# The down projection's Strassen parts in token-major form, with 512-column weight tiles

## The chip, the cores and the metric

The kernel runs on one core of a Trainium2 chip. The time is the device time of one execution in microseconds (us). Each kernel is executed several times, and the median is given. The engines of the core are TensorE (PE in the profile, its weight loads PEld), VectorE (DVE), ScalarE (ACT), GpSimd (POOL) and SyncE (SP), which issues most of the transfers.

## The reference

One decoder layer over 512 tokens of 2048 features in fp32: two token mixers (an MLA branch and a gated delta branch), merged and projected, then a SwiGLU channel mixer with 5632 hidden features, then a last RMS norm. What matters here is the end:

```python
h = _rmsnorm(x, norm_ffn[l]) * (1.0 + sc_f) + sh_f
gate, up = jnp.split(h @ w_gate_up[l], 2, axis=-1)
x = x + gt_f * ((jax.nn.silu(gate) * up) @ w_down[l])
return _rmsnorm(x, final_norm)
```

`gt_f` is one gate value for each of the 2048 output features, the same for all tokens.

## The kernel before, in words

Every fp32 operand is split into a high and a low part of type fp32r (ACT casts the high part, DVE subtracts it from the source for the low part), and a product is three matmuls: high by high, high by low, low by high. All of it accumulates in PSUM banks of 128 x 512 values. PE has a stationary operand of 128 x 128 and a moving one of up to 512 columns.

The channel mixer comes in these stages, in the order of PE. `gu0` and `gu_both` make the first gate and up columns. `big(s)`, s = 1 to 10, makes 512 gate and 512 up columns each, by a seven-product Strassen form in which weights and activations are split in two halves of rows (h) and columns: 16 units, 8 of a first pass with the products m1, m6, m7, m5 (24 matmuls of 128 x 512) and 8 of a second pass with m2, m4, m3 into the same eight PSUM banks (18 matmuls). The stationary operand is a 128 x 128 piece of an activation sum and the moving one a 512-column weight sum, so a result has tokens on its partitions and is called token-major. The second pass needs one weight sum of the first again; it goes through `s_dram`, stored by POOL and loaded by SP. `turned_a` transposes the activated results, between the matmuls of the second pass, to the feature-major form (features on partitions) that the down projection takes.

The down projection has 44 blocks of 128 rows. Blocks 0 to 15 ("ks=0") and 16 to 31 ("ks=1") go by Strassen, blocks 36 to 39 and 40 to 43 by plain feature-major sets (`dn`, called dn36 and dn40 below), blocks 32 to 35 are the last group. The order is dn36, ks=0, dn40, ks=1, last group. `strassen_down(ks, n)`, n = 0 to 3, is feature-major before the change: the stationary operand is a 128 x 128 piece of a weight sum, the moving one 256 columns (tokens) of an activation sum. Each of its 8 units (`strassen`, in `unit(k)`) loads a raw weight tile of 128 x 4 x 256, makes four weight sums on DVE (L1889), splits them and three raw parts (ACT L1897, DVE L1898) and issues 42 matmuls (the seven products, two halves, three each). Each of the two ks takes 32 units or 1344 matmuls. After a set, ACT scales the four results by the gate, with a sign for some (`gt_ffn`, `gt_neg`), and POOL adds them by an accumulating DMA to `x2_dram`, which holds the residual, feature-major.

The activation sums of a ks come from `sums_down(ks)`, a generator in a chain: for each quarter q it loads four tiles from `f_dram`, makes four sums (L1998) and seven high and low splits (L239, L240). `down_ready(ks, q)` draws them before the first matmul of a unit that needs them. The buffers of a quarter come free when the one before of the other ks is gone (`gone`, counted up in the last set of a ks, and `free(q)`).

The order of work is in the class `Driver`. A unit has loads (`start`), a preparation (`split`), matmuls, and work before and after (`pre`, `post`). The driver issues loads and preparations some units ahead. The chains (sums, outputs, activations) are stepped once after each GROUP = 12 matmuls (`pump`), or drawn when needed. PE, SP and POOL issue strictly in the order of the program; DVE and ACT instructions are put in order by the scheduler of the language, by their place and their operands.

The last group: `last_dn` runs the last Strassen set, brings `x2_dram` back into SBUF, and then makes the output in two halves. For tokens 0 to 255 it is feature-major (tiles dnl, 192 matmuls with 256 moving columns): the result is scaled and added (`add_gated`), the squares are summed over partitions by matmuls with a column of ones (hss), the norm's factor is spread by a diagonal matrix (hbc), `finished` writes `out`. For tokens 256 to 511 the residual is transposed (`turned`, tile x2T, 32 transposes), and `token_unit` makes 128 x 512 results (tile dnt, 96 matmuls), multiplies by the gate's row (L2240), adds to the residual (L2241), squares with a sum along the row (ACT L2242), multiplies by the norm's row (L2243); `scaled` applies the factor and writes `out_t`.

## Time and profile before

| | us |
|---|---|
| median of 3 runs | 2760.21 (2759.62 to 2762.45) |
| profiled execution | 2757.97 |
| its span | 2755.9 |
| PE busy | 2726.4 |
| DVE busy | 2017.6 |
| ACT busy | 1168.9 |
| POOL busy | 251.5 |

The span is the time from the first to the last instruction that the profiler recorded; the execution's own time is 2.07 longer. The stages on PE, from the first to the last start of their matmuls: `big` 1484.3 to 2264.0, dn36 2264.2 to 2309.4, ks=0 2309.6 to 2483.4, dn40 2483.5 to 2526.8, ks=1 2527.1 to 2692.5, dnl 2692.6 to 2715.5, the transposes to 2721.2, dnt to 2743.3, and then the end at 2755.9.

How lines of a profile are read here: a group of instructions stands as line, engine, operation, output tile <- input tiles, shapes and count, then the busy time in all and the mean duration of one in ns, then the engine's idle time ahead of them with what ended most of it. A line of the timeline begins with the start and the duration; an idle time just before it and its releaser stand in brackets. Nearly all matmuls are issued from one helper, L155, so they are told apart by their tiles: m is a Strassen product.

### The profile page before, as it was taken

The page shows a single profiled execution, that of the slowest core. Times are in us where ns is not written, and L with a number is a line of the kernel's source. Part 1 is how long each engine was busy: PE and PEld are TensorE (multiplying, and loading weights), DVE is VectorE, ACT ScalarE, POOL GpSimd, SP SyncE. Part 2 cuts the span into 40 slices and gives each one's busy share as a digit, 9 for nine tenths or more (in the row PEclk, how much of TensorE's full clock was granted, in tenths as well). Part 3 has the DMA queues.
Part 4 walks back from the last instruction along what each step waited for, and adds up shares of the span by engine and source line. Part 5 has one row for each costly group of instructions (what it writes and reads, how often), then busy time and mean ns, then how long its engine had stood idle before and what let it go on. Part 6 is the DMA issues. An engine that isn't in the chain of part 4 may idle for free.

```text
span 2755.9 us, 39855 instructions
## 1 busy us (share of the span) xinstructions
PE 2726.4 (99%) x14896; PEld 2348.2 (85%) x14896; DVE 2017.6 (73%) x3193; ACT 1168.9 (42%) x1649; POOL 251.5 (9%) x334
## 2 busy tenths in 40 slices
PE   9999999999999999999999999999999999999998
PEld 7888788888888888888999888888888888998997
DVE  8884657676967547785487877778877867878876
ACT  3443432542344343222373444444444445446545
POOL 0000011102100000001000000000000103113113
PEclk9999999999999999999999999999999999999999
DMA  9996556546754648885464565666565668469565
GB/s 350 313 364 203 152 162 179 190 146 182 211 150 153 203 143 287 306 298 195 158 182 146 189 202 199 207 213 201 200 210 191 213 204 193 115 194 207 123 190 173
DMA packets 308538, 557.93 MB, mean 202 GB/s; under 512 B 39956, under 2 KB 109748, under 8 KB 308216
## 3 DMA queue, kind: packets, MB, share of 16 engines
q1 hardware_dynamic: 259848, 461.09, 51.6%
q0 software_dynamic: 28704, 66.37, 9.3%
q10 hardware_dynamic: 19792, 27.92, 2.9%
q8 instruction: 116, 1.90, 0.3%
q14 instruction: 78, 0.64, 0.1%
HBM read 474.52 MB, written 80.76 MB: 201 GB/s over the span
## 4 chain that ended last, share of the span: by engine, by line
PE 94%; DVE 2%; DMA 2%; issue 1%; ACT 1%; SPq 0%; ACTq 0%; DVEq 0%; POOLq 0%
PE m L155 37%; PE wo L155 6%; PE gb L155 6%; PE v L155 4%; PE gu L155 3%; PE z L155 3%; PE ga L155 3%; PE ya L155 3%; PE k L155 3%; PE dn L155 3%; PE q L155 3%; PE yb L155 3%; PE s L155 3%; PE ckv L155 2%; PE cq L155 2%; PE qk L155 1%
## 5 line engine op out<-in xcount | busy, mean ns | idle before, releaser
L263 ACT CAST hi<-raw 128x1024 fp32r<-128x1024 f32 (+1 forms) x274 | 285.2, 1042 | 666.7 <-DMA raw<-in_w_in_dram 131.2
L264 DVE TENSOR_TENSOR lo<-raw,hi 128x1024 fp32r<-128x1024 f32 (+1 forms) x274 | 337.2, 1232 | 305.4 <-ACT hi L263 291.8
L1722 ACT CAST hi<-raws 128x512 fp32r<-128x512 f32 (+1 forms) x240 | 218.4, 910 | 329.0 <-PE m L155 270.4
L1723 DVE TENSOR_TENSOR lo<-raws,hi 128x512 fp32r<-128x512 f32 (+1 forms) x240 | 247.7, 1044 | 86.5 <-ACT hi L1722 86.3
L155 PE MATMUL m<-xl,hi 128*128 128x256 f32 x896 | 257.1, 287 | 3.8 <-DVE xl L240 3.8
L155 PE MATMUL m<-xh,hi 128*128 128x256 f32 x896 | 256.8, 287 | 3.7 <-ACT xh L239 2.3
L155 PE MATMUL m<-xh,lo 128*128 128x256 f32 x896 | 256.6, 286 | 0.8 <-DVE lo L1898 0.8
L435 DVE CUSTOM_DVE_ANT_0 rawm<-rawm,cbc 128x1024 f32<-128x1024 f32 x192 | 234.1, 1238 | 7.8 <-DMA rawm<-in_w_mod_dram 7.2
L155 PE MATMUL m<-hi,h2h 128*128 128x512 f32 x480 | 190.7, 397 | 0.4 <-DVE euvw L1740 0.3
L155 PE MATMUL m<-hi,h2l 128*128 128x512 f32 x480 | 187.2, 390 | 0.0
L155 PE MATMUL m<-lo,h2h 128*128 128x512 f32 x480 | 186.8, 389 | 0.0
L155 PEld LDWEIGHTS m<-xl,hi 128*128 128x128 f32 x896 | 175.0, 195 | 4.7 <-DVE xl L240 4.7
L155 PEld LDWEIGHTS m<-xh,hi 128*128 128x128 f32 x896 | 175.0, 195 | 4.4 <-ACT xh L239 2.7
L155 PEld LDWEIGHTS m<-xh,lo 128*128 128x128 f32 x896 | 175.2, 196 | 1.0 <-DVE lo L1898 1.0
L1722 ACT CAST hi<-sums 128x1024 fp32r<-128x1024 f32 x80 | 84.2, 1052 | 109.2 <-PE m L155 104.2
L1723 DVE TENSOR_TENSOR lo<-sums,hi 128x1024 fp32r<-128x1024 f32 x80 | 97.8, 1222 | 27.3 <-ACT hi L1722 26.8
L155 PE MATMUL wo<-mh,hi 128*128 128x512 f32 (+1 forms) x320 | 111.2, 347 | 0.0
L155 PE MATMUL wo<-mh,lo 128*128 128x512 f32 (+1 forms) x320 | 110.9, 347 | 0.0
L155 PE MATMUL wo<-ml,hi 128*128 128x512 f32 (+1 forms) x320 | 110.9, 347 | 0.0
L1897 ACT CAST hi<-sums 128x1024 fp32r<-128x1024 f32 x64 | 67.1, 1048 | 99.0 <-PE m L155 76.7
L1898 DVE TENSOR_TENSOR lo<-sums,hi 128x1024 fp32r<-128x1024 f32 x64 | 78.2, 1223 | 39.8 <-ACT hi L1897 39.6
L155 PEld LDWEIGHTS m<-hi,h2l 128*128 128x128 f32 x480 | 90.1, 188 | 19.5
(535 smaller groups left out, 7315.9 us busy)
## 6 DMA issues: line engine op xcount, KB each, us to landing
raws<-in_w_gate_up_dram SPq DMA_DIRECT2D x400, 256.0 KB, 3.5
rawm<-in_w_mod_dram SPq DMA_DIRECT2D x192, 512.0 KB, 5.5
raw<-in_w_in_dram SPq DMA_DIRECT2D x144, 512.0 KB, 4.7
raws<-in_w_down_dram SPq DMA_DIRECT2D x128, 256.0 KB, 4.1
raw<-in_w_o_dram SPq DMA_DIRECT2D x40, 512.0 KB, 4.6
s_dram<-raws POOLq DMA_DIRECT2D x80, 256.0 KB, 2.3
raws<-s_dram SPq DMA_DIRECT2D x80, 256.0 KB, 3.3
rawa<-in_w_in_dram SPq DMA_DIRECT2D x32, 512.0 KB, 4.4
```

The costliest lines, as they stand in the source:

```text
L155: return self.tc.keep_in_program_order(f(*args, **kwargs))
L263: nc.scalar.copy(hi[:], raw[:])
L264: (lo_eng or nc.vector).tensor_tensor(lo[:], raw[:], hi[:].bitcast(F32), ALU.subtract)
L435: r = nc.vector.tensor_tensor_reduce(raw, raw, c, 1.0, 0.0, ALU.mult, ALU.add, parts[:, k, half:half + 1])
L1722: nc.scalar.copy(hi[:], src)
L1723: nc.vector.tensor_tensor(lo[:], src, hi[:].bitcast(F32), ALU.subtract)
L1897: nc.scalar.copy(hi[:], src)
L1898: nc.vector.tensor_tensor(lo[:], src, hi[:].bitcast(F32), ALU.subtract)
```

## The change

`strassen` is now one function for gate/up and down. The down projection's Strassen parts take the form of `big`: activation sums stationary, 512-column weight sums moving, results token-major, two sets (n = 0, 1 of 1024 columns) per ks instead of four, 16 units each. The results are multiplied by the gate's row (`gate_row`, a broadcast load from `g_dram`) on DVE and go to a new array `z_dram` by POOL: plain stores for ks=0, accumulating ones for ks=1. `x2_dram` no longer receives them. In the last set (`last_down`) the residual comes back from `x2_dram`, all of it is transposed between the matmuls of the second pass (`turned_x2`), and the sums in `z_dram` are added by accumulating loads (`z_back`). The last group is token-major for all tokens: two sets of 512 columns for four token tiles each (`tm_set`), then eight `token_unit`s. Its weights have been multiplied by the gate's row beforehand: `gated_weights`, a chain started at `big(1)`, loads the 4 x 4 tiles, multiplies them on DVE, and stores them to `l_dram`. `finished`, the gate's negative and the columns of the last norm are gone, and there is one output array.

Of the diff, shortened:

```diff
-    def big(s):
-        g, u = 512 * s, DFF + 512 * s
+    def strassen(w, g, u, par, operand, ready, second_read, finish, freed, extra=None):
+        wg = w.rearrange("(h k p) n -> k h p n", h=2, p=P)
...
+        FIRST4 = [("m1", 0, 1, "m1"), ("m6", 0, 0, "m6"), ("m7", 1, 0, "m7"), ("m5", 1, 1, "m5")]
+        LAST3 = [("m2", 1, 0, "m1"), ("m4", 0, 0, "m7"), ("m3", 0, 1, "m5")]
...
+    def big(s):
...
+        return strassen(w_gu, 512 * s, DFF + 512 * s, s % 2, operand, ready, second_read, finish, freed,
+                        lambda k: turned_a(k - 1) if 1 <= k <= 4 else [])
+
+    def strassen_down(ks, n, extra=None):
+        tiles, rows = {}, []
+        def ready(q):
+            while made[ks] <= q:
+                drv.step(maker[ks])
+        def second_read(c, t, v, ps):
+            if c == "m2":
+                tiles[0, t] = S("y")
+                nc.vector.tensor_tensor(tiles[0, t][:], ps[:], rows[0][:], ALU.mult)
+            elif c == "m4":
+                tiles[1, t] = S("y")
+                nc.vector.tensor_tensor(tiles[1, t][:], v, ps[:], ALU.add)
+            else:
+                nc.vector.tensor_tensor(v, v, ps[:], ALU.add)
+        def finish(v, up1):
+            accum = dict(accum_op=ALU.add) if ks else {}
+            def out_(h, t, f, y):
+                c0 = 1024 * n + 512 * f
+                nc.gpsimd.dma_start(z_dram[2 * h + t, :, c0:c0 + 512], y, **accum)
+            for t in range(2):
+                out_(0, t, 0, tiles[0, t][:])
+            yield
+            for t in range(2):
+                nc.vector.tensor_tensor(tiles[1, t][:], tiles[1, t][:], rows[0][:], ALU.mult)
+                out_(1, t, 0, tiles[1, t][:])
+            yield
+            for h, x in enumerate((v, up1)):
+                for t in range(2):
+                    nc.vector.scalar_tensor_tensor(x[t], x[t], -1.0, rows[1][:], op0=ALU.mult, op1=ALU.mult)
+                    out_(h, t, 1, x[t])
+                yield
+        def freed(second, q):
+            if n == 1 and second:
+                down[ks][q] = None
+                gone[1 + ks] += 1
...
+        us = strassen(w_dn[2048 * ks:2048 * ks + 2048, :], 1024 * n, 1024 * n + 512, (1 + n) % 2, lambda c, q: down[ks][q][c],
+                      ready, second_read, finish, freed, extra)
+        with_pre([us[10]], lambda: rows.extend(gate_row(2 * n + f) for f in range(2)))
+        return us
+
+    def gate_row(n):
+        row = S("row")
+        side(row[:], g_dram[512 * n:512 * n + 512].partition_broadcast(P))
+        return row
+
+    def gated_weights():
+        for n in range(4):
+            row = gate_row(n)
+            for k in range(4):
+                w = S("wg")
+                side(w[:], w_dn[(LAST + k) * P:(LAST + k + 1) * P, 512 * n:512 * n + 512])
+                yield 4
+                tc.keep_in_program_order(nc.vector.tensor_tensor(w[:], w[:], row[:], ALU.mult))
+                side(l_dram[k, :, 512 * n:512 * n + 512], w[:])
+                w = None
+                yield 4
...
-    def strassen_down(ks, n):
...
-                        nc.scalar.activation(half_of(t, k), half_of(t, k), AF.Copy, scale=(gt_neg if f else gt_ffn)[:, k:k + 1])
-                    nc.gpsimd.dma_start(x2_dram[h, 2 * n + f], t[:], accum_op=ALU.add)
...
-    def strassen(w, c1, c0, products, ready, outputs, freed):
...
+        def x2_back(k):
+            n, h = divmod(k, 2)
+            for q in (2 * n, 2 * n + 1):
+                x2f[h, q] = S("x2")
+                side(x2f[h, q][:], x2_dram[h, q])
+        def turned_x2(k):
+            n, h = divmod(k, 2)
+            box = {}
+            def one(t, j):
+                if j == 0:
+                    box["ps"] = PS("x2T")
+                f = 4 * n + j
+                nc.tensor.transpose(box["ps"][:, tok(j)], half_of(x2f[h, f // 2], f)[:, tok(t)], ident)
+                if j == 3:
+                    x_ = xt[2 * h + t, n] = S("x2t")
+                    nc.scalar.copy(x_[:], box["ps"][:])
+                    if n < 2:
+                        z_back(2 * h + t, n)
...
+        def z_back(t, n):
+            nc.gpsimd.dma_start(xt[t, n][:], z_dram[t, :, 512 * n:512 * n + 512], accum_op=ALU.add)
+        def last_down():
+            weights = [last_weights(n, k0) for n in (2, 3) for k0 in (0, 2)]
+            for i, u in enumerate(strassen_down(1, 1, turned_x2)):
+                if 6 <= i < 14:
+                    with_pre([u], lambda i=i: x2_back(i - 6))
+                if i >= 12:
+                    with_pre([u], lambda i=i: reload_a(LAST + i - 12))
                 yield u
+                if i >= 12:
                     yield weights.pop(0)
...
+            for n in range(2):
+                us = tm_set("dnt", lambda k0, nk, n=n: gated(n, k0), 4, at,
+                            lambda ps, n=n: [summed(t, n, ps[t]) for t in range(NT)], late=True)
+                if n == 0:
+                    with_pre(us, last_rows)
+                yield from us
+            for t in range(NT):
+                for n in (2, 3):
+                    yield token_unit(t, n)
...
+        def summed(t, n, ps):
+            x_, sq = xt[t, n], S("sq")
+            nc.vector.tensor_tensor(x_[:], x_[:], ps[:], ALU.add)
+            nc.scalar.activation(sq[:], x_[:], AF.Square, accum_out=sf[:, t, n:n + 1])
+            (nc.gpsimd if n < 2 else nc.vector).tensor_tensor(x_[:], x_[:], norms[n][:], ALU.mult)
...
+        drv.add(gated_weights())
...
-        for n in range(4):
-            for k, u in enumerate(strassen_down(0, n)):
-                if (n, k) == (3, 2):
+        for n in range(2):
+            for i, u in enumerate(strassen_down(0, n)):
+                if (n, i) == (1, 10):
                     def start():
-                        for i in range(40, 44):
-                            reload_a(i)
+                        for k in range(40, 44):
+                            reload_a(k)
                         maker[1] = drv.add(sums_down(1))
...
-        for n in range(3):
-            yield from strassen_down(1, n)
-        yield from last_dn()
+        yield from strassen_down(1, 0)
+        yield from last_down()
```

More of the change, by code (lines that the diff above doesn't have):

```diff
@@ L349, in post @@
                     drv.hold()
-            return Unit(start, split, mms, pre, post, weight=weight, alone=alone)
+            return Unit(start, split, mms, pre, post, weight=weight, alone=alone, late=late and k0 + nk == kt)
         return [unit(k0) for k0 in range(0, kt, nk)]
@@ L1753, in after, with operand @@
+        return [unit(i) for i in range(16)]
+    def big(s):
+        tiles = {}
+        def operand(c, q):
+            if c in ("m1", "m2"):
+                return h2T[0][q if c == "m1" else 4 + q]
+            return h2T[1][4 + q] if c == "m4" else comb[q][c.replace("m", "x")]
+        def ready(q):
+            while xn[0] <= q:
+                drv.step(xc[0])
+        def second_read(c, t, v, ps):
+            if c == "m2":
                 tiles[0, t] = S("g0")
-                nc.scalar.activation(tiles[0, t][:], ps["m1"][t][:], AF.Silu)
@@ L1811, in block_kernel @@
+    LAST = 32
     turning = []
```

367 lines of the change are left out of this document (97 added, 270 removed).

## The prediction

> **What bounds the kernel now.** I read the page's totals and its chain of waits first, then each engine's busy time by stage, then what TensorE (PE) waits for in the stages that change, and last single instructions for their pitch.
>
> ```profile
> PE 2726.4 (99%) x14896; PEld 2348.2 (85%) x14896; DVE 2017.6 (73%) x3193; ACT 1168.9 (42%) x1649; POOL 251.5 (9%) x334
> PE 94%; DVE 2%; DMA 2%; issue 1%; ACT 1%; SPq 0%; ACTq 0%; DVEq 0%; POOLq 0%
> L155 PE MATMUL m<-xl,hi 128*128 128x256 f32 x896 | 257.1, 287 | 3.8 <-DVE xl L240 3.8
> L155 PE MATMUL m<-hi,h2h 128*128 128x512 f32 x480 | 190.7, 397 | 0.4 <-DVE euvw L1740 0.3
> ```
>
> PE is the bound: 99% busy, 94% of the chain that ends last. So an edit counts by the issue time that it takes from PE, and by the waits that it gives PE. The third and fourth rows show the shapes in question: the down Strassen's matmuls (three groups of 896, 2688 in all) take moving tiles of 256 columns, the gate and up projections' take 512. Their mean durations overlap; what counts is the distance from start to start.
>
> ```profile
> 2400.00 0.28 PE L155 MATMUL m<-xh,hi 128*128 128x256 f32 x1
> 2400.12 0.28 PE L155 MATMUL m<-xl,hi 128*128 128x256 f32 x1
> ```
> ```profile
> 1800.18 0.39 PE L155 MATMUL m<-hi,h2h 128*128 128x512 f32 x1
> 1800.41 0.39 PE L155 MATMUL m<-lo,h2h 128*128 128x512 f32 x1
> 1800.63 0.39 PE L155 MATMUL m<-hi,h2l 128*128 128x512 f32 x1
> ```
>
> A 256-column matmul costs 0.120 us, a 512-column one (1800.63-1800.18)/2, 0.225 to 0.227 with the rounding; the stages of such matmuls keep 0.2267. Two of the narrow ones cost 0.240: 13 ns more for the same columns. Now the stages (span and then busy time of PE, its weight loads, DVE, ACT and POOL, the granted clock, DMA share and GB/s):
>
> ```profile
> 1600.00:1700.00 100.00, 100.00 (x456) 82.83 (x455) 76.45 (x90) 44.71 (x56) 7.58 (x14) 1.00 0.60 199
> 2310.00:2484.00 174.00, 167.93 (x1346) 166.55 (x1345) 139.61 (x207) 84.73 (x116) 19.40 (x25) 0.96 0.61 162
> 2484.00:2527.00 43.00, 43.00 (x191) 35.63 (x190) 32.01 (x47) 27.61 (x45) 17.48 (x16) 1.00 1.05 224
> 2527.00:2692.00 165.00, 162.83 (x1342) 162.37 (x1341) 130.95 (x194) 78.39 (x107) 23.49 (x31) 0.99 0.62 161
> ```
>
> Row 1 is gate/up, the pattern the down projection is to take: PE full, VectorE (DVE) at 76%. Row 2 is the first down Strassen stage (K rows 0 to 2047, "ks=0"): 174.0-1346x0.120 = 12.5 us lost, though PE's idle time is only 6. Row 4 is ks=1: 165.0-1342x0.120 = 4.0 lost. The waits in between:
>
> ```profile
> PE m L155 <- DVE xl L240: 3.8, 4, 1.2
> PE m L155 <- ACT xh L239: 2.3, 2, 1.1
> PE m L155 <- ACT hi L1897: 1.4, 1, 1.4
> ```
> ```profile
> 2331.98 0.39 PE L155 MATMUL m<-xl,hi 128*128 128x256 f32 x1 [1.19 <-DVE xl L240]
> 2335.52 0.58 PE L155 MATMUL m<-xl,hi 128*128 128x256 f32 x1 [0.95 <-DVE xl L240]
> ...
> 2336.33 0.41 PE L155 MATMUL m<-xl,hi 128*128 128x256 f32 x1
> 2336.54 0.41 PE L155 MATMUL m<-xh,lo 128*128 128x256 f32 x1
> ```
>
> The operands xl and xh are the activation sums of the down Strassen, which DVE makes while the first units run. After such stalls matmuls follow at 0.21 instead of 0.120 for 4.9 us (the clock of row 2 is 0.96): a spell loses 4.9x(1-0.120/0.21) = 2.1 us beyond the stall.
>
> **The change part by part.**
>
> *Strassen on PE.* 2688x0.120 = 322.6 us become 1344x0.2267 = 304.7: **-17.9**. The weight load of 0.19 us still fits beside a matmul, as in gate/up. The Trainium skill ("TensorE: Matmul & The Clock Gate", Back-to-back issue gap) has the warm gap as N/2.4 ns plus 2.5 ns, which speaks against this gain: 1344 saved fixed parts of 2.5 ns would be an estimated 3.4 us. The rows above contradict it for this kernel's fp32r stream (13 ns).
>
> *Last group of K rows (4096 up).* Before: 192 narrow matmuls (23.0), the transposes' stage, 96 wide ones:
>
> ```profile
> 2715.50 0.28 PE L155 MATMUL dnl<-ah,wll 128*128 128x256 f32 x1
> 2715.62 1.29 PE L155 MATMUL x2T<-kc,x 128*128 128x128 f32 x10
> ...
> 2719.46 1.94 PE L155 MATMUL x2T<-kc,x 128*128 128x128 f32 x16
> 2721.16 0.48 PE L155 MATMUL dnt<-wlh,ah 128*128 128x512 f32 x1
> ```
> ```profile
> 2743.26 0.39 PE L155 MATMUL dnt<-wlh,al 128*128 128x512 f32 x1
> 2743.69 0.69 DVE L2240 TENSOR_TENSOR dn<-dnt,row 128x512 f32<-128x512 f32 x1 [0.20 <-PE dnt L155]
> 2745.04 0.68 DVE L2241 TENSOR_TENSOR x2t<-x2t,dn 128x512 f32<-128x512 f32 x1
> 2745.81 0.63 ACT L2242 ACTIVATE dn<-x2t 128x512 f32<-128x512 f32 x1
> ```
>
> 23.0+(2721.16-2715.62)+(2743.49-2721.16) = 50.9. After: 192x0.2267 = 43.5 and 64 transposes at (2721.16-2719.46)/16 = 0.106, 6.8: 50.3. **-0.6.** The transposes now stand between the last Strassen set's matmuls; each result needs an ACT copy, and ACT is under half busy there.
>
> *DVE in the two Strassen stages.* DVE works in order, so its spare time per unit says how fast the activation sums come. Pitches by the starts of consecutive instructions:
>
> ```profile
> 2310.81 1.23 DVE L1898 TENSOR_TENSOR lo<-sums,hi 128x1024 fp32r<-128x1024 f32 x1 [2.27 <-ACT hi L1897]
> 2311.96 0.69 DVE L240 TENSOR_TENSOR xl<-a,xh 128x512 fp32r<-128x512 f32 x1
> 2312.56 0.69 DVE L1889 TENSOR_TENSOR sums<-raws 128x512 f32<-128x512 f32 x1
> 2313.16 0.95 DVE L1898 TENSOR_TENSOR lo<-raws,hi 128x768 fp32r<-128x768 f32 x1
> 2314.03 0.42 DVE L1889 TENSOR_TENSOR sums<-sums,raws 128x256 f32<-128x256 f32 x1
> 2314.36 0.68 DVE L240 TENSOR_TENSOR xl<-a,xh 128x512 fp32r<-128x512 f32 x1
> ```
>
> 1.15 us for 1024 columns, 0.60 for 512, 0.87 for 768, 0.33 for 256. Before, a unit is 42 matmuls, 5.04 us, and takes DVE 0.60+2x0.33+0.87+1.15 = 3.28: 1.76 spare. After, a first-pass unit is 24 matmuls, 5.44 us, with three operations of 1024 and one of 512, 4.05: 1.39 spare. A second-pass unit is 18, 4.08 us, with 2.35: 1.73 spare. So the stage as a whole fits, as in row 1, but the spare time is smaller just where the sums are due. One quarter q of a ks's activations is four sums and seven splits: 11x0.60 = 6.6 us, used by first-pass units 2q and 2q+1, so quarter q is due 10.9q us after the stage's start (10.1q before).
>
> *Start of ks=0.* Before lost the 12.5. A walk down the changed program's DVE order with these pitches has q2's second operand ready 29.5 us after the start, due at 25.5: 4.0 late, some 2.2 again for q3, and two half-clock spells of 2.1: 10.4. The count of spare time bears that size out: before, three quarters are 33 operations, 19.9 us, against 6x1.76 = 10.6 spare in the first six units; 9.3 and two spells make 13.5, where 12.5 was lost. Bounds: nothing lost (the sums drawn into spare time), or 16, by that count for the new units: 19.9-6x1.39 = 11.6 and two spells. **-2.1** (-12.5 to +3.5).
>
> *Start of ks=1.* Before, the sums of quarters 0 to 2 came from the long end of ks=0 and the plain stage dn40 (row 3), and PE waited for none. The new order gives less room: the generator of the sums is stepped once every 12 matmuls, so every 2.7 us instead of 1.44, and the buffers of the old quarters come free only in the second pass of the last ks=0 set. By the changed order only q0 is made in dn40; the 19.9 us of q1 to q3 fall into the first six units, with their 8.3 spare. The rest, 11.6, comes late, with one half-clock spell: **+13.7**. Bounds: 9 (units 6 and 7 lend their spare time too, no spell) and 20 (all of it exposed). The skill's page on the clock gate (the same title, Part 1) has half rate only after an idle window of about 3.4 us; with three stalls each under that it would take no spell here, 11.6 instead of 13.7. The stalls above, about 1 us each, did bring one.
>
> *End of ks=1.* Before lost 4.0 there by a late weight DMA (the wait on `hi`). After, the loads of the last set are spread; but x2_dram's return, z_dram's accumulating loads, the reloaded activations and the last weights all come in units 6 to 15: 16.8 MB by the diff in about 50.6 us, 330 GB/s. The crowded 12 us before that late DMA:
>
> ```profile
> DMA packets 1828, 4.33 MB, mean 361 GB/s; under 512 B 257, under 2 KB 777, under 8 KB 1826
> ```
>
> Below that, but near. I take 1.5 lost: **-2.5** (-4 to +8: one late set of loads of two units' length).
>
> *Hidden work.* `gated_weights` is 16 DVE multiplies (9.7 us) over some 350 us of gate/up, where row 1 leaves DVE 23 us of each 100; uncovered it would cost those 9.7. The multiplies by the gate row replace ACT scalings and lie in second passes with 1.73 spare per unit. The sums' 32 transfers into z_dram go from POOL and are read back only in the last set.
>
> *Tail.* The last square starts one DVE multiply and one interleaved operation earlier (L2240 to L2241, 1.35 us): **-1.0** (-1.3 to 0).
>
> Sum: -17.9-0.6-2.1+13.7-2.5-1.0 = **-10.4**. Against the profiled execution (span 2755.9 plus 2.07, 2757.97) 2747.6; the median of the runs lies 2.2 above that execution, so **2750**.
>
> **The rivals.**
> *Smooth* (2728): DVE's sums slip into spare time, both starts lose nearly nothing (2 us in all): -17.9-0.6-12.5+2-2.5-1.0 = -32.5. For it: row 1's full PE at 76% DVE. Against: the 19.9 us of sums against 8.3 spare.
>
> *Slower by the sum's way through DRAM* (2768): the weight sum of a first pass is stored to s_dram by POOL and read back by the second pass, and POOL also carries dn40's accumulating transfers.
>
> ```profile
> x_dram<-y POOLq DMA_DIRECT2D x32, 256.0 KB, 8.0
> s_dram<-raws POOLq DMA_DIRECT2D x80, 256.0 KB, 2.3
> raws<-s_dram SPq DMA_DIRECT2D x80, 256.0 KB, 3.3
> ```
>
> If the store of unit 2 stands behind four such accumulates, it holds its buffer, and the next DVE sum behind it, for up to 8.0+2.3+3.3 = 13.6 us while q1 to q3 also wait in that order: 13.7+13.6+5 for two more half-clock spells = 32.3, against -24.1 for the other terms: +8.2. It decides for slower from a loss of 29.6 at this one place. For it: POOL's queue is in order, and those accumulates are the slowest issues. Against: POOL is 40% busy in row 3.
>
> *Same by crowding in the last set* (2760): loads of the last set come 10 us later in all than forecast. For it 330 against 361 GB/s; against, the window above is a burst of several queues, and the loads are issued units ahead.
>
> *The change doesn't do what it says* (2764): a wide matmul of the down stages costs nearly two narrow ones, 0.2375 instead of 0.2267, and 14.5 of the 17.9 stays away. For it: the overlap that a narrow pair lacks was seen in another stage only. Against: 0.2267 stands in gate/up with the same alternation of operands. (The skill's gap formula above comes to the same saving of 3.4.)
>
> **How the numbers follow.** Forecast 0.45, smooth 0.12, crowding 0.17, slower 0.23, not saved 0.03. 0.2% is 5.5 us, about what a measurement tells from no change: faster below 2754.7, slower above 2765.7. Faster 0.45+0.12, less 0.02 for the forecast's upper edge: 0.55; same 0.17+0.03-0.02: 0.18; slower 0.27 with the upper bounds of the other terms. Range: best bounds -17.9-0.6-12.5+9-4-1.3 = -27.3, 2733; worst -17.9-0.6+3.5+20+8 = +13, 2773: **2732 to 2774**; the forecast's own 2740 to 2756.
>
> **What would show it.** PE's 512-column matmuls in both Strassen stages at 0.2267; losses there of 10 and 14 us (window less count times pitch), waits on `x` sums (L240) in the first six units; the clock under 1 in the first 35 us of each; ks=1's last set without a wait on `hi`; the last group about 50 us; the last square some 1.3 us sooner after the last matmul. Wrong if ks=1's sums are ready before its first unit (then smooth), or if waits on weight sums or z loads lead the list.

## The result, and the profile after

The changed kernel takes 2825.2 us (median of 4 runs, 2820.6 to 2826.5) where the kernel before takes 2759.9 (4 runs): a ratio of 1.0234, 95% interval 1.0216 to 1.0251. The forecast was 2750 within 2732 to 2774, faster; the kernel became 65 us slower. The profiled execution has a span of 2823.0, 67.1 more than before. From the first matmul of each stage to the first of the next, in us:

| stage | before | after | at full pitch, after |
|---|---|---|---|
| up to `big` | 1484.3 | 1488.2 | |
| `big` (gate/up) | 779.9 | 792.1 | |
| dn36, dn40 | 45.4, 43.5 | 45.4, 43.5 | |
| ks=0 | 173.9 | 186.9 | 152.3 |
| ks=1 (after: with 64 transposes) | 165.5 | 210.6 | 159.1 |
| last group | 50.7 | 43.4 | 43.5 |
| from the last matmul's start to the end | 12.7 | 12.9 | |

The differences, +3.9, +12.2, +13.0, +45.0, -7.3 and +0.2, make 67.0. So the loss is in the two Strassen stages and, unexpected, in gate/up. The page's totals and chain, then a list of what PE waited for from gate/up to the end (total, times, longest):

```profile
PE 2727.9 (97%) x13478; PEld 2277.8 (81%) x13478; DVE 2013.9 (71%) x3110; ACT 1144.0 (41%) x1589; POOL 298.4 (11%) x420
PE 74%; DVE 9%; DMA 7%; issue 6%; ACT 1%; POOL 1%; SPq 0%; ACTq 0%; DVEq 0%; POOLq 0%
```
```profile
PE m L155 <- DVE euvw L1733: 19.9, 4, 8.9
PE m L155 <- DVE xl L240: 19.4, 6, 7.7
PE m L155 <- ACT xh L239: 13.7, 6, 3.9
PE x2T L155 <- ACT x2t L2148: 8.9, 2, 8.4
PE m L155 <- DVE lo L1717: 7.0, 5, 2.1
PE m L155 <- DVE sl L2009: 1.2, 1, 1.2
PE m L155 <- ACT sl L2007: 1.1, 1, 1.1
```

PE's share of the chain fell from 94 to 74%, and DMA and DVE came up. Two of the waits hardly stood in the kernel before: `euvw` (DVE's reads of the PSUM banks at the end of a first pass; 0.3 us in all before) and `x2t` (ACT's copy of the transposed residual; none before). The windows of the changed kernel say where (columns as in the prediction):

```profile
2326.00:2364.00 38.00, 26.19 (x102) 20.02 (x100) 27.81 (x33) 16.65 (x23) 7.74 (x9) 0.87 0.72 195
2364.00:2464.00 100.00, 97.09 (x414) 79.46 (x415) 81.12 (x99) 43.27 (x52) 15.55 (x29) 0.96 0.67 209
2464.00:2513.00 49.00, 38.62 (x160) 31.12 (x159) 27.87 (x36) 15.02 (x18) 1.09 (x3) 0.90 0.63 205
2556.00:2617.00 61.00, 42.66 (x161) 32.38 (x160) 46.30 (x59) 25.63 (x36) 8.63 (x12) 0.86 0.66 198
2617.00:2688.00 71.00, 71.00 (x315) 58.76 (x314) 56.45 (x68) 29.04 (x33) 10.98 (x15) 1.00 0.64 181
2688.00:2767.00 79.00, 59.63 (x266) 47.46 (x265) 40.73 (x52) 31.09 (x46) 22.04 (x36) 0.87 0.82 267
```

Row 5, the middle of ks=1, is what the change was to be everywhere: 315 matmuls in 71 us, 0.225 each, PE full. The start of ks=0 (row 1) loses 38-102x0.2267 = 14.9, the rest of its first set and the second's first pass (row 2) 6.1, the pass change of its second set (row 3) 12.7, the start of ks=1 (row 4) 24.5, and the last set (row 6, 202 matmuls and 64 transposes at 0.106) 26.4.

**The starts.** POOL, DVE and PE of the changed kernel at the first stall (start, duration; idle time before, and its releaser, in brackets):

```profile
2328.26 4.96 POOL L155 DMA_DIRECT2D x_dram<-y  x4 [6.17 <-ACT y L2061]
2331.19 2.60 POOL L155 DMA_DIRECT2D s_dram<-raws  x1
```
```profile
2334.30 1.22 DVE L1695 TENSOR_TENSOR sums<-raws,raws 128x1024 f32<-128x1024 f32 x1
2343.26 1.23 DVE L1695 TENSOR_TENSOR sums<-raws,raws 128x1024 f32<-128x1024 f32 x1 [7.75 <-DMA s_dram<-raws]
2344.41 1.28 DVE L1695 TENSOR_TENSOR raws<-sums,raws 128x512 f32<-128x512 f32 x2
2345.61 0.68 DVE L240 TENSOR_TENSOR xl<-a,xh 128x512 fp32r<-128x512 f32 x1
```
```profile
2346.35 0.79 PE L155 MATMUL m<-hi,xl 128*128 128x512 f32 x1 [7.72 <-DVE xl L240]
2346.94 0.63 PE L155 MATMUL m<-hi,xh 128*128 128x512 f32 x1
2347.37 0.63 PE L155 MATMUL m<-lo,xh 128*128 128x512 f32 x1
...
2351.23 0.39 PE L155 MATMUL m<-hi,xl 128*128 128x512 f32 x1
2351.46 0.39 PE L155 MATMUL m<-hi,xh 128*128 128x512 f32 x1
```

The store of a weight sum goes out in POOL's queue behind dn36's four accumulating transfers (`x_dram<-y`; the rows leave the number out of `x2_dram`). It reads one of five raw buffers; DVE's next weight sum wants that buffer and waits 7.75 us; the split xl for PE stands behind it in DVE's order. The list names xl, but what ended last is the store. After the stall the matmuls come at 0.43 for nine of them.

The start of ks=1 repeats it. There the profile names no releaser for DVE's wait ("issue"):

```profile
2571.72 1.22 DVE L1695 TENSOR_TENSOR sums<-raws,raws 128x1024 f32<-128x1024 f32 x1 [9.66 <-issue]
```

By the trace's times of issue and landing it is the store again: it went out at 2558.94 behind dn40's four accumulating transfers and landed at 2571.64. In both cases the four landed one after the other, some 2.7 us apart (2334.32 to 2342.31, 2562.46 to 2570.46), and the store about 1 us behind the last (2343.24, 2571.64).

**The pass change.** DVE and POOL in ks=0's second set:

```profile
2472.76 0.69 DVE L1695 TENSOR_TENSOR raws<-raws,raws 128x512 f32<-128x512 f32 x1 [4.16 <-DMA raws<-in_w_down_dram]
2475.34 0.69 DVE L1695 TENSOR_TENSOR raws<-raws,raws 128x512 f32<-128x512 f32 x1 [1.89 <-DMA raws<-in_w_down_dram]
2475.95 1.22 DVE L1717 TENSOR_TENSOR lo<-raws,hi 128x1024 fp32r<-128x1024 f32 x1
2477.09 1.28 DVE L1739 TENSOR_TENSOR euvw<-euvw,m 128x512 f32<-128x512 f32 x2
2478.28 2.47 DVE L1733 TENSOR_TENSOR euvw<-euvw,m 128x512 f32<-128x512 f32 x4
```
```profile
2455.38 0.54 POOL L155 DMA_DIRECT2D s_dram<-raws  x1 [4.41 <-DVE raws L1695]
2455.91 0.54 POOL L155 DMA_DIRECT2D ah<-a_dram  x1
...
2459.09 0.54 POOL L155 DMA_DIRECT2D ah<-a_dram  x1
```

The first pass's matmuls end at 2469.7. The reads that free their banks (L1739, L1733) need nothing more, but stand behind weight sums of later second-pass units (L1695) that wait for their loads. And the loads are late: POOL has sent the eight reloads of stored activations, which the program has at unit 10, in one go from 2455.9 on, while PE was still in the first pass. PE waited 8.9 us. Gate/up shows the same order, without the reloads, at 1776 us and at 1536 us, where the multiply by the gate's row (`wg`) stands between:

```profile
1536.72 0.69 DVE L1695 TENSOR_TENSOR raws<-raws,raws 128x512 f32<-128x512 f32 x1 [1.81 <-DMA raws<-in_w_gate_up_dram]
1537.33 1.22 DVE L1717 TENSOR_TENSOR lo<-raws,hi 128x1024 fp32r<-128x1024 f32 x1
1538.46 0.68 DVE L1893 TENSOR_TENSOR wg<-wg,row 128x512 f32<-128x512 f32 x1
1539.06 1.27 DVE L1739 TENSOR_TENSOR euvw<-euvw,m 128x512 f32<-128x512 f32 x2
```

**The last set.** The transfers of the changed kernel from 2735 to 2760, and ACT in that stretch:

```profile
DMA packets 3844, 8.84 MB, mean 354 GB/s; under 512 B 463, under 2 KB 463, under 8 KB 3844
```
```profile
2744.14 1.07 ACT L2148 COPY x2t<-x2T 128x512 f32<-128x512 f32 x2
2756.80 1.04 ACT L263 CAST hi<-raw 128x1024 fp32r<-128x1024 f32 x1 [4.05 <-DMA raw<-l_dram]
2757.75 1.07 ACT L2148 COPY x2t<-x2T 128x512 f32<-128x512 f32 x2
```

At 354 GB/s for 25 us the casts of the last weights wait for their loads, the copy of the transposed tiles waits behind a cast, and the next transposes wait 8.4 us for the bank.

### The profile page after: what moved, and what is told of

It is laid out like the page before. It is cut to its first block, busy times and chain, and to the rows that moved or that the text cites. A ratio compares the mean times of both kernels' runs of the same rounds, so it can differ in the third digit from the quotient of the medians.

```text
span 2823.0 us, 37070 instructions
## 1 busy us (share of the span) xinstructions
PE 2727.9 (97%) x13478; PEld 2277.8 (81%) x13478; DVE 2013.9 (71%) x3110; ACT 1144.0 (41%) x1589; POOL 298.4 (11%) x420
## 4 chain that ended last, share of the span: by engine, by line
PE 74%; DVE 9%; DMA 7%; issue 6%; ACT 1%; POOL 1%; SPq 0%; ACTq 0%; DVEq 0%; POOLq 0%
PE m L155 30%; PE wo L155 6%; PE gb L155 6%; PE v L155 4%; PE k L155 3%; PE s L155 3%; PE yb L155 3%; PE q L155 3%; PE z L155 3%; PE gu L155 2%; DMA raws<-in_w_down_dram 2%; PE ya L155 1%; PE qk L155 1%; DMA raw<-in_w_in_dram 1%; DVE lo L1717 1%
## 5 line engine op out<-in xcount | busy, mean ns | idle before, releaser
L1716 ACT CAST hi<-raws 128x1024 fp32r<-128x1024 f32 (+1 forms) x336 | 305.7, 910 | 534.9 <-PE m L155 358.8
L1717 DVE TENSOR_TENSOR lo<-raws,hi 128x1024 fp32r<-128x1024 f32 (+1 forms) x336 | 345.8, 1042 | 118.5 <-ACT hi L1716 117.8
L155 PE MATMUL m<-hi,xh 128*128 128x512 f32 x448 | 182.4, 407 | 27.5 <-DVE euvw L1733 13.8
L155 PE MATMUL m<-hi,xl 128*128 128x512 f32 x448 | 181.4, 405 | 19.4 <-DVE xl L240 19.4
L155 PE MATMUL m<-lo,xh 128*128 128x512 f32 x448 | 180.8, 403 | 7.0 <-DVE lo L1717 7.0
L1695 DVE TENSOR_TENSOR sums<-raws,raws 128x1024 f32<-128x1024 f32 x112 | 136.5, 1219 | 40.7 <-DMA raws<-in_w_down_dram 11.7
L1695 DVE TENSOR_TENSOR raws<-raws,raws 128x512 f32<-128x512 f32 x112 | 76.5, 688 | 89.3 <-DMA raws<-in_w_gate_up_dram 59.3
L155 PEld LDWEIGHTS m<-hi,xh 128*128 128x128 f32 x448 | 88.0, 196 | 49.6 <-ACT xh L239 16.8
L155 PEld LDWEIGHTS m<-hi,xl 128*128 128x128 f32 x448 | 87.6, 196 | 41.6 <-DVE xl L240 23.1
L155 PEld LDWEIGHTS m<-hi,h2h 128*128 128x128 f32 x480 | 90.1, 188 | 25.3 <-DVE euvw L1733 7.8
```

The source lines that it names most:

```text
L155: return self.tc.keep_in_program_order(f(*args, **kwargs))
L1695: add = lambda o, x, y: nc.vector.tensor_tensor(o, x, y, ALU.add)
L1716: nc.scalar.copy(hi[:], src)
L1717: nc.vector.tensor_tensor(lo[:], src, hi[:].bitcast(F32), ALU.subtract)
```

## The experiments

Theories at the start: (1) the store's queue makes the stalls at the starts; (2) DVE's order makes those at the pass changes; (3) POOL's side loads run ahead and make weights late; against these the prediction's own reason, (4) DVE's load of activation sums and their slow generator. First each alone. A time without an interval is of a single execution, and so is every stage's time; these are read to some 4 us, as ten executions of one kernel (e6 below) lie between 2758.3 and 2765.6.

**e1_store_act.** The down stages' stores from ACT's queue:

```diff
-                side(s_dram[par, k], r[:, 0, :])
+                (store or side)(s_dram[par, k], r[:, 0, :])
...
-                      ready, second_read, finish, freed, extra)
+                      ready, second_read, finish, freed, extra, nc.scalar.dma_start)
```

> Only the queue changes that stores the weight sums of the two down Strassen stages to s_dram: ACT's in place of POOL's. Queue theory: in the changed kernel each of the two stages starts with a stall of PE of 7.7 us, because the store of a weight sum stands in POOL's queue behind four accumulating transfers and DVE waits for the buffer that it holds. Without those transfers ahead of it both stalls of 7.7 go, and some of the shorter ones after them: 15 to 30 us less than the changed kernel, 2795 to 2810. Rival, DVE's load of activation sums (the prediction's reason): DVE has too little spare time in the first six units, whatever queue the store takes: both starts still lose 20 us and more, and the time stays within 5 us of 2825.

2809.0, 16.2 less. The stalls of 7.7 became 1.8 and 1.5. ks=0 fell from 186.9 to 176.4, ks=1 only from 210.6 to 206.9: later waits at the start of ks=1 (5.3 us on xh) took part of the place. Told by the first set of a stage (the time from its first to its last matmul's start, less 335x0.2267), the loss fell from 21.4 to 13.9 in ks=0 and from 24.8 to 19.9 in ks=1. Theory 1 holds; it is not the whole of the starts. The Trainium skill ("Trainium Kernel Development and Optimization", Key Constraints) says that transfers from all three queues run on the same 16 DMA engines and that issuing from several engines only saves issue time. The measured 16 us show a second thing that a queue decides: what stands ahead in it.

**e2_pin.** The weight sum of a second-pass unit may not be scheduled ahead of what the program has before it:

```diff
-                add(r[:, 0, :], r[:, 0, :], b[:])
+                tc.keep_in_program_order(add(r[:, 0, :], r[:, 0, :], b[:]))
```

> Only the order on DVE changes: the weight sum of a second-pass unit may not move ahead of what the program has before it, so the reads of the PSUM banks at the end of the first pass come ahead of the sums of the units behind them. Order theory: the PE waits for those reads (4.4 and 1.7 us in gate/up, 8.9 us in ks=0, 4.9 us in ks=1) stand behind sums that wait for weight loads; with the order changed they go and nothing takes their place: 20 to 25 us less, about 2802. Rival, late loads: the loads are late in any case, and PE waits as long for the split weights of the first second-pass unit as it did for the reads: under 8 us less, over 2817.

2788.7, 36.5 less: more than expected. Gate/up is back at 781.0, the waits on euvw are gone, ks=0 is at 173.6, ks=1 at 196.5 (the wait of 8.4 us before the transposes went too, which the theory had not named). DVE at the same pass change:

```profile
2453.33 1.22 DVE L1717 TENSOR_TENSOR lo<-raws,hi 128x1024 fp32r<-128x1024 f32 x1 [2.46 <-ACT hi L1716]
2454.48 1.28 DVE L1739 TENSOR_TENSOR euvw<-euvw,m 128x512 f32<-128x512 f32 x2
2455.67 2.66 DVE L1733 TENSOR_TENSOR euvw<-euvw,m 128x512 f32<-128x512 f32 x4
2458.25 0.69 DVE L1695 TENSOR_TENSOR raws<-raws,raws 128x512 f32<-128x512 f32 x1
```

The reads come ahead of the sum, and nothing waits for a load between.

**e3_sp.** Gate rows, reloads and the residual's return through SP, in the program's place, the reloads one block per unit:

```diff
-                side(x2f[h, q][:], x2_dram[h, q])
+                load(x2f[h, q][:], x2_dram[h, q])
...
-                side(aT[k][i][:].bitcast(F32), a_dram[k - 32, i])
+                load(aT[k][i][:].bitcast(F32), a_dram[k - 32, i])
...
+                if n == 1 and 9 <= i < 13:
+                    with_pre([u], lambda i=i: reload_a(31 + i))
```

> The loads of the gate's rows in the down stages, of the stored activations and of x2_dram go to SP's queue, at the places where the program has them, in place of POOL's; the four reloads for dn40 are spread over four units. Crowding theory: POOL issues these loads long before the units that they belong to, some 2 MB at once, and the weight loads beside them land late: with SP's order the stalls at the pass change of ks=0's second set (1.6 and 9.1 us) and before and at that of ks=1's second set (1.7, 2.2 and 5.3 us) go, 15 to 20 us less, about 2807. Rival, order on DVE: the reads of the banks still stand behind sums of later units, and those loads wait for SP just as long: within 6 us of 2825. A third way: loads in SP's queue hold up the weights behind them, and the time rises.

2798.1, 27 less, more than the 15 to 20 expected: ks=0 at 180.0, ks=1 at 190.3. The pass-change waits shrank (8.9 to 4.9, 4.9 to 1.5) but did not go, and the wait before the transposes fell from 8.4 to 1.3. Theory 3 holds beside theory 2.

**e4_nogate.** The chain `gated_weights` left out:

```diff
-        drv.add(gated_weights())
...
-            return [(lambda r: r[:], l_dram[k0:k0 + 2, :, 512 * n:512 * n + 512].rearrange("k p n -> p k n"))]
+            return plain(w_dn, LAST + k0, 2, 512 * n, 512)
```

> The chain that multiplies the last group's weights by the gate's row is left out, and the last group takes its weights from w_down without the gate: that part of the result lacks the gate. If that chain's loads, stores and multiplies are what costs gate/up its 12 us, the stage goes back to 780 us and the time to some 2813. Rival: the stage's stalls come from the order of DVE at the pass change, which the chain only meets by chance: the stage keeps 5 us or more of the 12.

2811.7, and gate/up at 780.5: all of its 12 us go. With e2_pin the chain stays and 11 of the 12 us go too (PE keeps a wait of 1.2 us on an activation sum of gate/up that e4 does not have). So its 16 multiplies are hidden but for about 1 us; what cost was the order of DVE that the scheduler chose with them in the program, at pass changes that they stand next to. What in the chain led the scheduler to it was not tested.

**e8_pump.** The chains stepped every 6 matmuls from ks=0 on:

```diff
-                if self.count >= GROUP:
-                    self.count -= GROUP
+                if self.count >= self.group:
+                    self.count -= self.group
...
+                        drv.group = GROUP // 2
```

> The changed kernel with the chains stepped every 6 matmuls in place of 12 from ks=0 on and nothing else. By the prediction's reason (the sums of ks=1 are late because their generator is stepped half as often) ks=1's first set loses 8 to 14 us less than the 24 that it loses in the changed kernel, about 2813. By the queue theory the first stall there is the store's and stays, and only the shorter waits shrink: 0 to 6 us less, 2819 to 2825.

2803.3, 21.8 less, more than either expectation: ks=0 at 177.4, ks=1 at 199.6. PE's waits on xl and xh fell from 33.1 to 3.7 us. The prediction's reason is real, at both starts. The first set of ks=1 loses 11.7 us in place of 24.8; these 13 us are within what was expected. That of ks=0 loses 13.1 in place of 21.4, which was not expected. At each start one stall stays, of 4.8 and 7.2 us, on split weights.

**Together.** The three edits (e5), with the faster chains (e6), and with single edits taken back or changed:

> The three edits of the first kernels together: ACT's queue for the stores, the pinned second-pass sums, SP's queue for the side loads. If the three causes are separate, their gains add but for what two of them share (the pass changes in the second sets): the changed kernel less 16, less 36, less some 15 for the loads, about 2757, near the kernel before. If they are one cause seen three times, the time stays near the best of them, 2785 to 2790.

> As the kernel with the three edits, and the chains are stepped every 6 matmuls in place of 12 from ks=0 on, so as often in time as before the change. The prediction's reason for the start of ks=1: stepped twice as often, the sums of more quarters are made before the stage starts, and 8 to 14 us go from that start. Rival: the buffers of a quarter come free too late for that, or a faster chain takes DVE's time at a worse place: within 4 us of the kernel with the three edits.

> As the kernel with the three edits and the faster chains, but the weight sums of the down stages are stored from SP's queue in place of ACT's. If the stores on ACT hold up the casts of the activation sums behind them (PE waits for xh, 2 to 5 us each at both starts with the stores on ACT), those waits go: 5 to 12 us less than the same kernel with the stores on ACT. Rival: the casts wait for sums that DVE makes late, whatever ACT stores: within 3 us. A loss: SP's loads of the next units' weights stand behind a store that waits for DVE.

> As the kernel with three edits and faster chains, less the edit of the stores: they go from POOL again. If the store behind POOL's accumulating transfers costs by itself (some 16 us alone), the two starts show a first wait of 4 to 8 us again and the time is 10 to 18 us above 2760.7. Rival: with the chains faster the sums are ready and the store's lateness is covered: within 5 us.

> As the kernel with three edits and faster chains, less the edit of the side loads: POOL issues them ahead again. If the early loads cost by themselves, the last set shows its waits again (transposes on ACT's copy up to 8 us, split weights 2 us each) and the time is 10 to 16 us above 2760.7. Rival: with the order on DVE pinned they do no harm: within 5 us.

| kernel | us | ks=0 | ks=1 |
|---|---|---|---|
| e5_three | 2772.0 | 167.4 | 184.4 |
| e6_three_pump | 2760.7, ratio to before 1.0001 (0.9991 to 1.0011) | 164.5 | 178.7 |
| e7_spstore (e6, stores on SP) | 2792.9, 1.0118 (1.0101 to 1.0134) | 173.3 | 197.8 |
| e12_pin_sp_pump (e6, stores on POOL) | 2770.8 | 170.2 | 182.5 |
| e13_pin_acts_pump (e6, side loads on POOL) | 2772.6 | 165.6 | 189.3 |

e5 lies 53 below the changed kernel, less than the sum of the three alone (80): the causes overlap. e6 is 11 below e5, 8.6 of it in the two stages (5.7 in ks=1, where 8 to 14 were expected). Taking one edit back costs 10 (stores) and 12 us (side loads), so both still count. Without the stores' edit the first waits at the starts are back (5.7 and 6.5 us), as expected. Without that of the side loads the transposes wait 0.4 us and not the 8 expected; the waits on split weights grew in their place, from 12.5 to 19.9 us. On SP the stores are worse than on POOL: SP's next weight loads stand behind a store that waits for DVE (DVE's wait for weights with its first-pass sums is 37.1 us in all, 19.2 in e6). With all four edits e6 is level with the kernel before.

**What is left.** e6 still loses 12.2 us in ks=0 and 19.6 in ks=1 against full pitch.

*e10_layout* (x2_dram as 16 x 128 x 512, so that accumulating transfers move 2 KB rows):

```diff
-                nc.gpsimd.dma_start(x2_dram[:, k // 2, :, 256 * (k % 2):256 * (k % 2) + 256].rearrange("h p n -> p h n"),
-                                    t[:].rearrange("p (h n) -> p h n", h=2), accum_op=ALU.add)
+                nc.gpsimd.dma_start(x2_dram[k], t[:], accum_op=ALU.add)
```

> As the kernel with three edits and faster chains, but x2_dram is laid out by feature block with all 512 tokens in a row, so that the plain stages' accumulating transfers move 2 KB rows in place of 1 KB rows, and the last set loads 16 tiles of that form. If those transfers crowd the DMA engines at the ends of dn36 and dn40, where DVE waits for the s_dram store's buffer (6.1 us in all) and for weights, each of them lands in some 5 us in place of 7, the starts of both Strassen stages lose 3 to 8 us less, and the time falls to 2753 to 2758, below the kernel before. Rival: what those starts wait for is DVE's own backlog and the size of the pieces does not matter: within 2 us of 2760.7. A loss: the last set's loads come in lumps of four.

2762.1, ratio 1.0008 (0.9998 to 1.0018): no gain; the size of the rows is not it.

*e14_spread* (`yield 8` after each of those transfers in the last sets, `yield 3` after each into z_dram, rows from unit 4):

> As the kernel with three edits and faster chains, and three transfers are moved in time: the accumulating transfers of the last set of dn36 and of dn40 go out one every 8 chain steps, so over the first units of the Strassen stage behind; the down sums go to z_dram one every 3 steps; the gate's rows are loaded from unit 4 on in place of unit 10. If the rest of the loss is weights and s_dram stores that land late among these transfers (PE waits of 2.3 and 1.6 us at the start of ks=1, 4.0 us at that of its second set, 1.9 us in ks=0 behind a gate row that lands late), 8 to 14 us go and the time is 2747 to 2753, below the kernel before. Rival: the DMA engines are full in these stretches whatever the order, and the waits move to the next units: within 3 us of 2760.

2761.8, 1.0009 (1.0000 to 1.0018): the waits moved. The one on the gate's row and that of 4.0 us at the start of ks=1's second set went; one of 2.4 us came at 2366, one of 1.8 before the transposes, and that at the start of ks=1 grew from 1.6 to 3.9.

*e15_no_store* and *e16_no_accum* take a suspect away (shortened):

```diff
-                side(s_dram[par, k], r[:, 0, :])
+                if store is None:
+                    side(s_dram[par, k], r[:, 0, :])
...
-            for dst, src in (((box["r"][:, 0, :], s_dram[par, k]), (box["r"][:, 1, :], wg[k, 1][:, u:u + 512]),
+            for dst, src in (((box["r"][:, 0, :], s_dram[par, k] if store is None else wg[k, 0][:, u:u + 512]), (box["r"][:, 1, :], wg[k, 1][:, u:u + 512]),
```
```diff
-            accum = dict(accum_op=ALU.add) if ks else {}
+            accum = {}
...
-                                    t[:].rearrange("p (h n) -> p h n", h=2), accum_op=ALU.add)
+                                    t[:].rearrange("p (h n) -> p h n", h=2))
```

> As the kernel with three edits and faster chains, but the down stages' weight sums are not stored and reloaded: the second pass loads raw weights of the same size in their place, so that part of the result is wrong, and DVE, PE and the loads do as much as before. If the round trip of the sums is what the two stages still lose (some 30 us over matmuls at full pitch), most of the waits at the starts go and the time falls by 10 to 20 us, to 2741 to 2751. Rival: DVE's own load at the starts, or the loads of weights, hold PE as long: less than 5 us.

> As the kernel with three edits and faster chains, but the plain stages' results and those of ks=1 overwrite x2_dram and z_dram in place of being added by the transfer: the same bytes go out, and the residual and ks=0's sums are missing from the result. If accumulating transfers crowd the DMA engines at the starts and at ks=1's second set, those waits shrink and the time falls by 6 to 15 us. Rival: the size of the traffic, not its kind, or DVE's load: less than 4 us.

2743.1 (ks=0 159.7, ks=1 164.9) and 2747.5 (159.7, 171.4): 17.6 and 13.2 less. Both count, and overlap, as each alone takes ks=0 from 164.5 to 159.7.

*e17_copy* keeps the store and frees its buffer: ACT copies the sum into the small buffer that held the second operand, and the store reads that; *e18_copy_spread* has e14's spreading too:

```diff
...
+                    nc.scalar.copy(b[:], r[:, 0, :])
+                    store(s_dram[par, k], b[:])
```

> As the kernel with three edits and faster chains, but ACT copies each weight sum of the down stages into the small buffer that the sum's second operand leaves, and the store goes from there: the raw buffer that DVE waits for no longer waits for the store. Leaving the store out gave 17.6 us. If that was the buffer held by the store, most of it comes without leaving it out: 8 to 15 us, 2746 to 2753, below the kernel before. Rival: it was the store's traffic beside the weight loads, or ACT's copy ahead of its casts costs as much: within 4 us of 2760.7.

> The copy before the store, and the three transfers moved in time as in the kernel that spread them. If the buffer held was what kept the spreading from showing a gain, the accumulating transfers' 13 us come back in part here: 3 to 8 us below the kernel with the copy alone. Rival: they cost what they cost wherever they stand: within 3 us of it.

e17: 2752.9, ratio to before 0.9971 (0.9961 to 0.9980), ks=0 160.9, ks=1 175.5. e18: 2756.3, 0.9986 (0.9976 to 0.9995): the spreading gives nothing here either. So about 8 of the store's 17.6 us, net of what the copy costs, were the buffer that it held; DVE waits for no store any more. The list of PE's waits in e17, from gate/up to the end:

```profile
PE m L156 <- DVE lo L1723: 6.7, 5, 4.0
PE m L156 <- DVE xl L241: 3.8, 4, 1.5
PE m L156 <- ACT xh L240: 3.4, 2, 1.8
PE m L156 <- DVE sl L2015: 1.2, 1, 1.2
PE x2T L156 <- ACT x2t L2154: 0.8, 1, 0.8
```

16 us where the changed kernel had 71. e17 is faster than both kernels, by 0.3% than the one before. Its longest wait (4.0) is on split weights at the start of ks=1's second set, while the first set's sums go out to z_dram.

## Why the prediction was wrong, point by point

The forecast was 10 us less and the span grew by 67, so 77 us separate them. The step that failed is that the stages were taken to run inside "as in row 1", with no term for the pass changes: 11 of the 12.2 us in gate/up and the 12.7 in ks=0 came there, with a part of the 26.4 of the last set. The rest are terms that were sized too low: 25 us in the last set, 21 at the two starts.

- *Strassen on PE, -17.9*: right. Where PE does not wait, the pitch is 0.2267 in both stages (row 5 above; in ks=0 the starts at 2419.67 and 2420.81 are five matmuls apart), so the 13 ns per matmul are saved, and the rival that they are not is out. By the Trainium skill's 2.5 ns ("TensorE: Matmul & The Clock Gate", Back-to-back issue gap) it would have been an estimated 3.4; the rows differ from it, for this stream.
- *Last group, -0.6*: right in its matmuls (43.4) and transposes, but these were costed as if a copy by ACT were free because ACT is under half busy. In the rows above the copy stands in ACT's order behind a cast that waits for a load, and PE waited 8.4 us for it.
- *Start of ks=0, 10.4 lost*: 14.9 to 2364 and 6.1 more to 2464, over the upper bound of 16. The walk down DVE's order took every transfer as landed in time. DVE's wait for the store's buffer was 7.75, and it stands in that order; the rival of the store was thought of for ks=1 alone. With the store on another queue (e1) the first set loses 13.9, so late sums were real and near the size forecast.
- *Start of ks=1, 13.7 lost*: 24.5, over the upper bound of 20. The mechanism named, late sums by a generator that is stepped half as often, was there (e8: 13 us less), and the rival that was to make it slower, the store behind dn40's accumulating transfers, was there beside it (DVE waited 9.66 us for it, where the rival had 13.6; e1: 5 us less). Forecast and rival were treated as alternatives; both came, and overlapped, as the loss stayed under the 32.3 that the rival added up.
- *Pass changes*: the step that failed most. The prediction had no term for them; "the stage as a whole fits, as in row 1" carried the whole inner part of the stages. What it overlooked is that nothing in the program held DVE's reads of the banks ahead of the sums of later units: that they came in time in gate/up before was the scheduler's choice. e2 pins the sums and takes 36.5 us away (11 in gate/up, 13 in ks=0 and 14 in ks=1, less 2 as gate/up began later in that execution).
- *Hidden work, 0 for `gated_weights`*: the cover named (DVE 76% busy) was there, and 12.2 us were lost all the same, all but about 1 by the order that the chain brought about (e2, e4). An average over a stage does not see a point where DVE decides.
- *End of ks=1, 1.5 lost*: 26.4 in the last set. Demand was worked out right as an average over units 6 to 15 (330 GB/s; in e17, where PE hardly waits, those units move 17.6 MB in 51.7 us, 341 GB/s), but POOL sent its part as early as its queue allowed. The crowding rival had the place, at 10 us. DVE's order had a part here as well: with the side loads on SP (e3) 6 us of the loss are left, with the order pinned (e2) 11.
- *Tail, -1.0*: +0.2. The last square began 3.3 us after the last matmul's start, where it was 2.5 before. The last addition came not after the last matmul but after DVE had gone through the earlier token tile's reciprocal root and norm multiply:

```profile
2810.16 0.39 PE L155 MATMUL dnt<-wlh,al 128*128 128x512 f32 x1
2811.26 0.68 DVE L2209 TENSOR_TENSOR x2t<-x2t,norm 128x512 f32<-128x512 f32 x1
2812.13 0.69 DVE L2207 TENSOR_TENSOR x2t<-x2t,dnt 128x512 f32<-128x512 f32 x1
```

- *Range*: its upper end added the bounds of the terms there were. Some 29 of the 77 us lie in places with no term (ahead of and in gate/up, and ks=0's pass change), and both starts and the last set went over their bounds. The matmuls were summed right. That e17, at 2752.9, is near the forecast of 2750 is luck in part: it has five edits more, and loses 25 us in the two stages (8.6 and 16.4) where the forecast had 25.6, but not where the forecast had them.

Open: the 3.9 us before gate/up. That part has no changed instruction of PE; gate/up began between 1485.4 and 1490.0 among these kernels, and no run was made for it. Of e6's remaining loss e15 and e16 name two causes; what DVE's own load makes of the rest was not separated.

## What to carry to other kernels

Taking a pattern over from a stage where it runs at full pitch is only safe if the queues, the order on the other engines and the free buffers come with it: ask at each change of pass or stage what stands ahead of the instruction that frees a bank, and what that waits for. A transfer that a buffer's release depends on should not share an in-order queue with slow ones, and should not hold a scarce buffer; side loads on a queue with nothing else to wait for can go out long before the place where the program has them, as the eight reloads did here. Where an instruction on an idle-looking engine frees PE's bank, cost its queue, not its duration.

## What the runs showed of the hardware

In the changed kernel eight spells of matmuls at 0.43, 66 in all, cost 66x0.2 = 13 us beyond the waits; they lasted 2.6 to 5.1 us and began 0.6 to 2.3 us behind a stall of 3 us or more; stalls of 1.1 to 1.7 us that stood alone or in pairs, as in gate/up, brought none. A long stall is not needed, though: in e17 two stalls of 1.8 and 1.0 us within 4 us brought a spell of 5.5 us, and two of 1.6 and 1.0 within 4 us brought none. The Trainium skill ("TensorE: Matmul & The Clock Gate", Part 1) gives half rate after at least one idle window of about 3.4 us, and full rate after about 3.4 us busy: the spells' length is of that size, the idle time needed was less here.

The traces' records of the granted clock show what tells the pairs apart. In all 18 traces every change of the clock falls on a grid of 3.413 us (to 3 ns). From gate/up to the end, of the windows of that grid with the full clock, none of the 6476 in which PE was idle, by the profile, for less than 1.65 us was followed by half clock, all 72 with 1.96 us or more were, and 11 of the 20 between. A window at half clock was followed by the full clock when PE was idle in it for 0.58 us or less, and by another one at half when it was idle for 0.65 us or more. The pair of 1.8 and 1.0 us put 1.97 us into one window; the pair of 1.6 and 1.0 fell into two.

A store of 256 KB that took 2.4 us to land over the whole program (median) took 7.4 (the median of three; the one that DVE waited for took 12.0) in the stretch behind accumulating transfers on its queue, which took 7.1:

```profile
x_dram<-y POOLq DMA_DIRECT2D x8, 256.0 KB, 7.1
s_dram<-raws POOLq DMA_DIRECT2D x3, 256.0 KB, 7.4
```
